# A first projection that reads a feature-major copy of x, in a two-block transformer kernel

## The chip, the cores and the metric

The kernel runs on one core of a Trainium2 chip. Its engines are TensorE (PE; its weight loads stand apart as PEld), VectorE (DVE), ScalarE (ACT), GpSimd (POOL) and SyncE (SP), which here issues the DMAs. The metric is the device time in microseconds (us) of one execution, as the median of several runs; shorter is better.

## The reference, cut to what matters

One sequence of 256 tokens of 1024 features passes two blocks. The part around the change is the first layer of the first block, in which a norm, one wide product and two attentions follow each other:

```python
def rms_norm(x, g):
    xf = x.astype(f32)
    y = xf * lax.rsqrt(jnp.mean(xf * xf, axis=-1, keepdims=True) + EPS)
    return (y * g.astype(f32)).astype(x.dtype)

def even_layer(x, g_norm, w_in, b_f, w_out):
    z = rms_norm(x, g_norm) @ w_in      # q, k, v, gate of 16 "a" heads, 16 forget gates, q, k, v, gate of 16 "b" heads
    ...
def forgetting_attention(q, k, v, log_f):        # the "a" heads
    c = jnp.cumsum(log_f, axis=1).transpose(0, 2, 1)
    ...
        s = s + c[:, :, q0:e, None] - c[:, :, None, :e]
        p = jax.nn.softmax(jnp.where(causal, s, NEG), axis=-1)
```

`log_f` is the log of the sigmoid of the forget product plus a bias. Each head's output is multiplied by its gate (gate times sigmoid of gate) and the result goes through `w_out` and is added to x. After it come a retention layer (block one) and, in block two, a state-space mixer, a sliding-window attention and a gated feed-forward layer.

## The kernel before, in words

A framework schedules the instructions: each engine's list is fixed when the kernel is built, and an engine works through its list in order. The program is one long row of TensorE products on weights that stream in. The class `Weights` loads tiles of 128 x 1024 float32 (512 KB) in the order of use, five raw tiles at a time, and splits each in two: ScalarE casts the raw tile into `wh` (L73), VectorE subtracts it into `wl` (L78). The casts run two tiles ahead of the products, and there are six `wh` and six `wl` tiles. Activations have two parts as well (`xTh`, `xTl`, feature-major: 128 features by 8 feature tiles by 256 tokens), and a product is the sum of three: h by h, h by l, l by h.

The start: `load_x` loads x (four pieces of 256 KB) and the first weight tile; the gain row is spread over 128 partitions by two products (L598) into two PSUM banks. `norm_transposed` forms the squares' sums (ScalarE and VectorE), the factor r with a power on GpSimd, and `xn` = x r g on VectorE (L215). Sixteen TensorE transposes (L235) turn it into PSUM, from where ScalarE casts `xTh` (L242) and VectorE forms `xTl` (L243). `first_xs` is the first projection (v of the first 8 "a" heads, four weight tiles): 48 products of 512 columns, 32 at L289 and 16 with the weights' lower parts at L296. Two of the first four lower weight parts are made by GpSimd. The forget product (24 products of 16 rows, L250 to L252) follows.

Then per half (`hf`) of an attention and per group of four heads (`i`): a q, a k and a gate projection (`proj_ws`: 48 products of 256 columns each), q scaled by ScalarE (L664), k copied by VectorE (L667), the gate through ScalarE's tanh (L670) and VectorE (L671). Each of two pairs of heads then takes: scores (L338) in the two PSUM banks `at`; a masked minimum on VectorE (`masked_min`, L346 and L348); exponentials on ScalarE (`exps`, L355 and L356); a scaling on VectorE (L685, L686); transposes of p (L362) into one of the two PSUM banks `pt`, emptied by ScalarE (`p_transposed`, L364); p by v (L372) in bank `py`.

The mask of the "a" heads comes from the forget gates by a chain: bias and log sigmoid (L630 to L635), a scan over the tokens on VectorE (L637), a reordering copy on GpSimd (L639), a DMA to memory (`c_dram`), a DMA per pair that spreads it over the partitions (`m`), and two additions of the causal mask on GpSimd (L648, L649).

Beside this, VectorE, ScalarE and GpSimd make tables for block two's state space (`trig`, `pw_r`, `m`, L389 to L531), from the parameters `ssm_par`; ScalarE's sines need another function table than its exponentials, and each change is an `ACT_TABLE_LOAD`.

## Time and profile before

| what | value |
|---|---|
| device time, median of 3 runs | 811.92 us |
| lowest and highest run | 810.0 and 812.02 us |
| span of the profiled execution | 810.7 us |
| TensorE products: busy, share of the span | 780.7 us, 96% |
| VectorE | 560.7 us, 69% |
| ScalarE | 408.3 us, 50% |
| GpSimd | 237.2 us, 29% |

The span runs from the first to the last recorded instruction of one profiled execution; the page gives no device time of that execution, so the three runs' times stand beside it. A busy share is an average over the whole program and tells nothing of a single stage.

### The profile page before, as it was taken

The page shows a single profiled execution, that of the slowest core. Times are in us where ns is not written, and L with a number is a line of the kernel's source. Part 1 is how long each engine was busy: PE and PEld are TensorE (multiplying, and loading weights), DVE is VectorE, ACT ScalarE, POOL GpSimd, SP SyncE. Part 2 cuts the span into 40 slices and gives each one's busy share as a digit, 9 for nine tenths or more (in the row PEclk, how much of TensorE's full clock was granted, in tenths as well). Part 3 has the DMA queues.
Part 4 walks back from the last instruction along what each step waited for, and adds up shares of the span by engine and source line. Part 5 has one row for each costly group of instructions (what it writes and reads, how often), then busy time and mean ns, then how long its engine had stood idle before and what let it go on. Part 6 is the DMA issues. An engine that isn't in the chain of part 4 may idle for free.

```text
span 810.7 us, 13533 instructions
## 1 busy us (share of the span) xinstructions
PE 780.7 (96%) x5114; PEld 682.1 (84%) x5114; DVE 560.7 (69%) x1013; ACT 408.3 (50%) x680; POOL 237.2 (29%) x274
## 2 busy tenths in 40 slices
PE   7989999999999999999999999989798999999996
PEld 5978997998997789898989887876577999999886
DVE  6987668678778468585766757698849856565433
ACT  5766565457455355344444355736645544443331
POOL 4662111013604212120202006853653322221110
PEclk9999999999999999999999999999999999999999
DMA  7687544644744757453636494852243765555431
GB/s 284 222 270 234 172 165 131 208 150 154 238 161 133 234 186 254 154 188 124 208 119 194 151 334 152 301 195 85 81 127 110 235 200 177 189 183 181 156 130 53
DMA packets 47427, 146.46 MB, mean 181 GB/s; under 512 B 5361, under 2 KB 11777, under 8 KB 47362
## 3 DMA queue, kind: packets, MB, share of 16 engines
q1 hardware_dynamic: 47362, 145.60, 54.5%
q8 instruction: 40, 0.66, 0.3%
q14 instruction: 25, 0.20, 0.1%
HBM read 137.70 MB, written 7.88 MB: 180 GB/s over the span
## 4 chain that ended last, share of the span: by engine, by line
PE 82%; DVE 5%; POOL 4%; issue 3%; ACT 3%; DMA 3%; SPq 0%; POOLq 0%; DVEq 0%; ACTq 0%
PE bpp L274 12%; PE bpp L275 12%; PE bpp L278 12%; PE bpp L251 9%; PE bpp L250 9%; PE bpp L252 9%; PE bat L252 3%; PE bat L251 3%; PE bat L250 3%; PE bpy L372 2%; PE bat L338 2%; PE bpt L362 1%; PE bpp L289 1%; DVE wl L78 1%; POOL wl L78 1%
## 5 line engine op out<-in xcount | busy, mean ns | idle before, releaser
L78 DVE TENSOR_TENSOR wl<-wraw,wh 128x1024 fp32r<-128x1024 f32 x211 | 276.5, 1321 | 114.9 <-ACT wh L73 114.9
L73 ACT CAST wh<-wraw 128x1024 fp32r<-128x1024 f32 (+1 forms) x233 | 238.6, 1045 | 190.0 <-PE bpp L251 54.1
L251 PE MATMUL bpp<-xTl,wh 128*128 128x256 f32 (+1 forms) x680 | 193.3, 284 | 0.0
L250 PE MATMUL bpp<-xTh,wh 128*128 128x256 f32 (+1 forms) x680 | 193.1, 284 | 0.0
L252 PE MATMUL bpp<-xTh,wl 128*128 128x256 f32 (+1 forms) x680 | 192.9, 284 | 0.0
L251 PEld LDWEIGHTS bpp<-xTl,wh 128*128 128x128 f32 (+1 forms) x680 | 127.3, 187 | 2.6 <-issue 1.9
L250 PEld LDWEIGHTS bpp<-xTh,wh 128*128 128x128 f32 (+1 forms) x680 | 127.3, 187 | 1.8 <-issue 1.3
L252 PEld LDWEIGHTS bpp<-xTh,wl 128*128 128x128 f32 (+1 forms) x680 | 127.3, 187 | 1.0 <-issue 0.8
L274 PE MATMUL bpp<-wh,xTh 128*128 128x512 f32 (+1 forms) x288 | 110.9, 391 | 0.8 <-ACT xTh L242 0.8
L275 PE MATMUL bpp<-wl,xTh 128*128 128x512 f32 (+1 forms) x288 | 109.6, 385 | 0.0
L78 POOL TENSOR_TENSOR wl<-wraw,wh 128x1024 fp32r<-128x1024 f32 x22 | 57.7, 2624 | 62.9 <-ACT wh L73 62.9
L278 PE MATMUL bpp<-wh,xTl 128*128 128x512 f32 (+1 forms) x288 | 74.2, 382 | 0.0
L274 PEld LDWEIGHTS bpp<-wh,xTh 128*128 128x128 f32 x288 | 54.5, 190 | 13.3 <-ACT xTh L242 1.7
L275 PEld LDWEIGHTS bpp<-wl,xTh 128*128 128x128 f32 x288 | 54.5, 189 | 11.1 <-DVE wl L78 0.6
L278 PEld LDWEIGHTS bpp<-wh,xTl 128*128 128x128 f32 x288 | 52.2, 188 | 11.1
L274 PE MATMUL bpp<-wh,yh 128*128 128x512 f32 x128 | 50.5, 400 | 0.0
L275 PE MATMUL bpp<-wl,yh 128*128 128x512 f32 x128 | 50.4, 396 | 0.0
L252 PE MATMUL bat<-xTh,wl 128*128 128x256 f32 x160 | 45.1, 282 | 0.0
L250 PE MATMUL bat<-xTh,wh 128*128 128x256 f32 x160 | 45.1, 282 | 0.0
L251 PE MATMUL bat<-xTl,wh 128*128 128x256 f32 x160 | 45.0, 281 | 0.0
L1119 POOL TENSOR_TENSOR gr<-gr,Rh 128x512 f32<-128x512 f32 x10 | 14.3, 1427 | 75.5 <-ACT th L1118 75.5
L278 PE MATMUL bpp<-wh,yl 128*128 128x512 f32 x128 | 35.6, 395 | 0.0
(380 smaller groups left out, 1312.3 us busy)
## 6 DMA issues: line engine op xcount, KB each, us to landing
wraw<-in_w_o SPq DMA_DIRECT2D x40, 512.0 KB, 4.3
wraw<-in_w_gate SPq DMA_DIRECT2D x22, 512.0 KB, 3.8
wraw<-in_w_up SPq DMA_DIRECT2D x22, 512.0 KB, 4.2
wraw<-in_w_dn SPq DMA_DIRECT2D x22, 512.0 KB, 3.7
wraw<-in_w_v SPq DMA_DIRECT2D x16, 512.0 KB, 4.6
wraw<-in_w_g SPq DMA_DIRECT2D x16, 512.0 KB, 4.4
wraw<-in_w_q SPq DMA_DIRECT2D x12, 512.0 KB, 4.1
wraw<-in_w_va SPq DMA_DIRECT2D x8, 512.0 KB, 6.6
```

Of the source, the lines that this page charges most:

```text
L73: i = nc.scalar.copy(h[:, :n], r[:, :n])
L78: self.lows.append(eng.tensor_tensor(lo[:, :n], r[:, :n], h[:, :n].bitcast(F32), op=ALU.subtract))
L250: T.matmul(ps, lh, rh, start=first, stop=False)
L251: T.matmul(ps, lh, rl, start=False, stop=False)
L252: T.matmul(ps, ll, rh, start=False, stop=last)
L274: T.matmul(ps, lh[:, k0 + k, st], wh, start=first and k == 0, stop=False)
L275: T.matmul(ps, lh[:, k0 + k, st], wl, start=False, stop=False)
L278: T.matmul(ps, ll[:, k0 + k, st], wh, start=False, stop=last and k == n - 1)
L289: m = T.matmul(ps[t], xp[:, k, st], tiles[k // 2][0][:, 512 * (k % 2):512 * (k % 2) + 512], start=xp is xTh and k == 0, stop=False)
L338: i = T.matmul(ps[j][:, o], q[rows, qs], k[rows, ks], start=True, stop=True)
L372: i = T.matmul(o[64 * j:64 * j + 64], v[:, b, vc], src, start=b == 0, stop=b == 1)
L1119: G.tensor_tensor(two(gr), two(gr), rep2(Rh), op=ALU.mult)
```

## The change

The host hands over x a second time, feature-major (`xT`), and the gain as a column per feature tile (`g_col`). ScalarE forms `xTh` = xT g and VectorE `xTl` directly from it, without the norm's factor, and the transposes, the gain's spreading and the row-major norm at the start are gone. The factor of a token, r, is made beside the products: squares of xT on ScalarE behind the fifth cast, sums on VectorE, two products with one column (L693 of the new kernel), the power on GpSimd; a row of factors `R` on every partition comes from two products (L706) behind the first q projection and a ScalarE copy (L708). v takes r in its scaling (L724), the forget product, q, k and the gate are multiplied by R on VectorE (L650, L730, L733, L741), in all passes of both attentions; q's scaling thereby leaves ScalarE.

The first eight weight tiles are loaded into the space of `yh`, `yl`, a ninth into the ordinary raw tiles, the first in two halves between pieces of xT. `first_xs` goes weight tile by weight tile over both token tiles. No lower part of the first projection is made by GpSimd. The forget product uses bank `py`. The row-major x (1 MB) and the masks are loaded behind later weight tiles, and `ssm_par` behind the thirteenth, so the tables begin later. Behind this layer the order of the instructions hardly changes.

```diff
 class Weights:
...
+        self.issued, self.given, self.casts = [], {}, []
...
     def load(self):
         ap = self.jobs[self.loads]
+        n = ap.shape[1]
+        if self.loads in self.given:
+            r = self.given.pop(self.loads)
+        else:
+            r = self.raw.tile([P, 1024], F32, tag="raw", name="wraw")
+        parts = 2 if self.loads == 0 else 1
         self.loads += 1
-        r = self.raw.tile([P, 1024], F32, tag="raw", name="wraw")
-        self.nc.sync.dma_start(r[:, :ap.shape[1]], ap)
+        for i in range(parts):
+            sl = slice(i * n // parts, (i + 1) * n // parts)
+            m = self.nc.sync.dma_start(r[:, sl], ap[:, sl])
+            if i == 0 and parts > 1:
+                self.between()
+        self.issued.append(m)
...
-        i = nc.scalar.copy(h[:, :n], r[:, :n])
+        if not self.done:
+            nc.scalar.copy(h[:, :n // 2], r[:, :n // 2])
+            i = nc.scalar.copy(h[:, n // 2:n], r[:, n // 2:n])
+        else:
+            i = nc.scalar.copy(h[:, :n], r[:, :n])
+        self.casts.append(i)
...
+    def issue_after(self, n, i):
+        self.tc.add_manual_dep(i.ins, self.issued[n].ins.name, NOSYNC, reason="order")
...
-    g_row = nrm.tile([P, D], F32, tag="gain", name="g_row")
-    nc.sync.dma_start(g_row[:1, :], a["even_norm"])
+    warm = const.tile([P, 1], F32, name="warm")
+    A.copy(warm, ones[:, :1])
...
+    g_col = const.tile([P, 8], F32, name="g_col")
+    nc.sync.dma_start(g_col, a["even_norm"])
+    xT = [nrm.tile([P, 4, S], F32, tag="gain", name=f"xT{h}") for h in range(2)]
     def load_x(t):
-        for h in range(XH):
-            sl = slice(h * D // XH, (h + 1) * D // XH)
-            nc.sync.dma_start(x[t][:, sl], a["x"][t * P:(t + 1) * P, sl])
-    load_x(0)
+        w.issue_after(10, nc.sync.dma_start(x[t], a["x"][t * P:(t + 1) * P, :]))
+    def load_xT(k, n=2):
+        nc.sync.dma_start(xT[k // 4][:, k % 4:k % 4 + n, :], a["xT"][:, k:k + n, :])
+    load_xT(0, 1)
...
-            w.plan(xs("w_v" + m, hf), SH[0] if m + str(hf) != "a0" else 2)
+            w.plan(xs("w_v" + m, hf), SH[0])
...
-    w.load()
-    load_x(1)
+    early = [ypool.tile([P, 16, S], F32R, tag=n, name="early")[:].rearrange("p a b -> p (a b)").bitcast(F32)
+             for n in ("yh", "yl")]
+    w.given = {j: early[j // 4][:, 1024 * (j % 4):1024 * (j % 4) + 1024] for j in range(8)}
+    w.between = lambda: load_xT(1, 1)
+    for k in (2, 4, 6):
+        w.load()
+        load_xT(k)
+    for _ in range(5):
+        w.load()
...
-    def first_xs(mid):
-        tiles = [w.next() for _ in range(4)]
+    def first_xs():
         ps = [bank("pp"), bank("pp")]
-        for t in range(2):
-            st = slice(t * P, (t + 1) * P)
-            for g in range(0, 8, 2):
-                for xp in (xTh, xTl):
-                    for k in range(g, g + 2):
-                        m = T.matmul(ps[t], xp[:, k, st], tiles[k // 2][0][:, 512 * (k % 2):512 * (k % 2) + 512],
-                                     start=xp is xTh and k == 0, stop=False)
-                        if t == 0 and xp is xTh and k == 1:
-                            mid(m)
-        for t in range(2):
-            st = slice(t * P, (t + 1) * P)
-            for k in range(8):
-                T.matmul(ps[t], xTh[:, k, st], tiles[k // 2][1][:, 512 * (k % 2):512 * (k % 2) + 512],
-                         start=False, stop=k == 7)
+        tiles = []
+        def part(g, xp, j, first=False, last=False):
+            for k in range(g, g + 2):
+                for t in range(2):
+                    T.matmul(ps[t], xp[:, k, t * P:(t + 1) * P],
+                             tiles[k // 2][j][:, 512 * (k % 2):512 * (k % 2) + 512],
+                             start=first and k == g, stop=last and k == g + 1)
+        for g in range(0, 8, 2):
+            tiles.append(w.next())
+            part(g, xTh, 0, first=g == 0)
+            part(g, xTl, 0)
+            if g:
+                part(g - 2, xTh, 1)
+        part(6, xTh, 1, last=True)
         return ps
...
-        nc.sync.dma_start(sp, a["ssm_par"])
+        w.issue_after(12, nc.sync.dma_start(sp, a["ssm_par"]))
...
-    g_even = [bank("at") for h in range(2)]
-    for h in range(2):
-        T.matmul(g_even[h], ones[:1, :], g_row[:1, h * 512:(h + 1) * 512], start=True, stop=True)
-    norm_transposed(0, g_even, xTh, xTl, "e0", eng=V)
-    def second_tile(after):
-        norm_transposed(1, g_even, xTh, xTl, "e1", KE, None, after)
+    for k in range(8):
+        xk = xT[k // 4][:, k % 4, :]
+        A.activation(xTh[:, k, :], xk, AF.Copy, scale=g_col[:, k:k + 1])
+        V.scalar_tensor_tensor(xTl[:, k, :], xk, g_col[:, k:k + 1], xTh[:, k, :].bitcast(F32),
+                               op0=ALU.mult, op1=ALU.subtract)
...
-            ps = bank("pp")
+        def forget_product():
+            ps = bank("py")
             wf = [y.rearrange("p (k c) -> p k c", c=16) for y in w.next()]
...
+            V.tensor_tensor(az, ps[:16, :S], R[:16, :], op=ALU.mult)
...
+        rh = []
+        R = evc.tile([P, S], F32, name="Re")
+        def square_sums():
+            sq = [ev.tile([P, 512], F32, tag=n, name="sq_e") for n in ("q", "k", "q", "k")]
+            for j in range(4):
+                i = A.activation(sq[j], xT[j // 2][:, 2 * (j % 2):2 * (j % 2) + 2, :].rearrange("p a b -> p (a b)"),
+                                 AF.Square, scale=1.0 / math.sqrt(D))
+                tc.add_manual_dep(i.ins, w.casts[4].ins.name, NOSYNC, reason="order")
+            V.tensor_tensor(sq[0], sq[0], sq[1], op=ALU.add)
+            V.tensor_tensor(sq[2], sq[2], sq[3], op=ALU.add)
+            V.tensor_tensor(sq[0], sq[0], sq[2], op=ALU.add)
+            V.tensor_tensor(sq[1][:, :S], sq[0][:, :S], sq[0][:, S:], op=ALU.add)
+            return sq[1][:, :S]
+        def norm_factors(sm):
+            pr = bank("pt")
+            rs = []
+            for t in range(2):
+                T.matmul(pr[:, t:t + 1], sm[:, t * P:(t + 1) * P], ones[:, :1], start=True, stop=True)
+            for t in range(2):
+                rs.append(rstd_from([pr[:, t:t + 1]], EPS, "e"))
+                rh.append(evc.tile([P, 1], F32, name=f"rh{t}"))
+                V.tensor_scalar(rh[t], rs[t], 0.5, None, op0=ALU.mult)
+            return rs
+        def factor_row(rs, after):
+            pr = bank("pt")
+            for t in range(2):
+                rb = ev3.tile([P, P], F32, tag="s", bufs=5, name="rb_e")
+                V.tensor_copy(rb, rs[t].to_broadcast([P, P]))
+                i = T.matmul(pr[:, t * P:(t + 1) * P], rb, ident, start=True, stop=True)
+                tc.add_manual_dep(i.ins, after.ins.name, NOSYNC, reason="order")
+            A.copy(R, pr[:, :S])
...
-                ps = proj_xs(xTh, xTl, 8) if mi or hf else first_xs(second_tile)
+                if mi or hf:
+                    ps = proj_xs(xTh, xTl, 8)
+                else:
+                    ps = first_xs()
+                    pf = forget_product()
+                    rs = norm_factors(square_sums())
+                    p0 = proj_ws()
+                    factor_row(rs, last_mm[-1])
...
-                    A.mul(v[:, t, :], ps[t], 0.5)
+                    A.mul(v[:, t, :], ps[t], rh[t])
...
-                    A.mul(q.rearrange("p a b -> p (a b)"), ps, -0.125)
+                    V.scalar_tensor_tensor(q, rows(ps), -0.125, rep2(R), op0=ALU.mult, op1=ALU.mult)
...
-                    V.tensor_copy(k.rearrange("p a b -> p (a b)"), ps)
+                    V.tensor_tensor(k, rows(ps), rep2(R), op=ALU.mult)
+                    if not (mi or hf or i):
+                        w.issue_after(6, nc.sync.dma_start(masks, a["c_masks"]))
+                        for t in range(2):
+                            load_x(t)
...
-                    A.activation(gs, ps, AF.Tanh, scale=0.5)
-                    V.scalar_tensor_tensor(gs, gs, 1.0, ps, op0=ALU.add, op1=ALU.mult)
+                    gr = ev.tile([P, 2 * S], F32, tag="gr", bufs=1, name="gr_e")
+                    V.tensor_tensor(rows(gr), rows(ps), rep2(R), op=ALU.mult)
+                    A.activation(gs, gr, AF.Tanh, scale=0.5)
+                    V.scalar_tensor_tensor(gs, gs, 1.0, gr, op0=ALU.add, op1=ALU.mult)
...
     a["x"] = c(i["x"][0][ORDER])
-    a["even_norm"] = c(i["even_norm"][0])
+    a["xT"] = c(a["x"].T.reshape(8, P, S).transpose(1, 0, 2))
+    a["even_norm"] = c(i["even_norm"][0].reshape(8, P).T)
```

**TensorE at the start.** These are TensorE's first rows before; `bpp` is the projection's PSUM bank, and a count is of like instructions in a row.

```order
L598 MATMUL bat<-g_row,ones 128x512 x2
L235 MATMUL bpt<-ident,xn 128x128 x8
L289 MATMUL bpp<-wh,xTh 128x512 x2
L289 MATMUL bpp<-wh,xTl 128x512 x2
L235 MATMUL bpp<-ident,xn 128x128 x4
L289 MATMUL bpp<-wh,xTh 128x512 x2
L289 MATMUL bpp<-wh,xTl 128x512 x2
L235 MATMUL bpy<-ident,xn 128x128 x4
```

The same place of the changed kernel:

```order
L308 MATMUL bpp<-wh,xTh 128x512 x4
L308 MATMUL bpp<-wh,xTl 128x512 x4
L308 MATMUL bpp<-wh,xTh 128x512 x4
L308 MATMUL bpp<-wh,xTl 128x512 x4
L308 MATMUL bpp<-wl,xTh 128x512 x4
L308 MATMUL bpp<-wh,xTh 128x512 x4
L308 MATMUL bpp<-wh,xTl 128x512 x4
L308 MATMUL bpp<-wl,xTh 128x512 x4
```

Transposes and the gain's products are gone, each weight tile is used for both token tiles (four products per part), and a tile's lower part comes in one tile later.

**ScalarE at the pairs of the first half.** Before, ScalarE's rows from the first tanh to the copies of the second pair's transposed p; `trig` are the sines of the tables, `s,dn<-s,nm` the exponentials.

```order
L461 ACT_TABLE_LOAD
L461 ACTIVATE trig<-trig 128x1024 x2
L73 CAST wh<-wraw 128x1024
L355 ACT_TABLE_LOAD
L355 ACTIVATE s,dn<-s,nm 128x128 x2
L73 CAST wh<-wraw 128x1024
L356 ACTIVATE s,dn<-s,nm 128x256
L664 ACTIVATE q<-bpp 128x512
L356 ACTIVATE s,dn<-s,nm 128x256
L355 ACTIVATE s,dn<-s,nm 128x128
L356 ACTIVATE s,dn<-s,nm 128x256
```

In the changed kernel, these are the rows of the third pair of heads up to the copy (L385) that empties the bank of the second pair's first transposed p:

```order
L376 ACTIVATE s,dn<-s,nm 128x128
L377 ACTIVATE s,dn<-s,nm 128x256
L482 ACT_TABLE_LOAD
L482 ACTIVATE trig<-trig 128x1024
L376 ACT_TABLE_LOAD
L376 ACTIVATE s,dn<-s,nm 128x128
L377 ACTIVATE s,dn<-s,nm 128x256
L86 CAST wh<-wraw 128x1024 x2
L482 ACT_TABLE_LOAD
L482 ACTIVATE trig<-trig 128x1024
L347 CAST yh<-o 128x256
L385 COPY pT<-bpt 128x384
```

The two sines have moved from ahead of the first pair's exponentials to between and behind those of the third pair, with three table loads, and the copy of p stands behind them.

**VectorE between the first and the third pair.** In the changed kernel, a piece of VectorE's list behind the second pair's masked minimum (`ISA s,nm`), up to the third pair's; of before, nothing of the tables' `trig` stands between these pairs, since it lies ahead of the first.

```order
L410 SCALAR_TENSOR_TENSOR trig<-trig 128x512 x2
L92 TENSOR_TENSOR wl<-wraw,wh 128x1024
L741 TENSOR_TENSOR gr_e<-bpp,Re 128x512
L506 TENSOR_TENSOR sm_t_1690<-pw_r,pw_i 128x16
L507 TENSOR_TENSOR sm_t_1691<-pw_i,pw_r 128x16
L525 TENSOR_TENSOR sm_fr<-sm_u_1717,sm_u_1718 128x16
L92 TENSOR_TENSOR wl<-wraw,wh 128x1024
L756 RECIPROCAL rd<-dn 128x2
L414 SCALAR_TENSOR_TENSOR trig<-trig 128x512 x2
```

The tables' work now lies on VectorE among the pairs' own instructions.

## Rows read from the trace of the kernel before

A row of a timeline gives: start in us, duration, engine, line, operation, out<-in, shapes, count, and in brackets the idle time before it and what ended it.

**Rows 1.** The profile's page: its first line, the products' row under heading 1 (busy time, share of the span, instructions), and under heading 4 the shares by engine of the chain of work that ended last.

```profile
span 810.7 us, 13533 instructions
...
PE 780.7 (96%) x5114; PEld 682.1 (84%) x5114; DVE 560.7 (69%) x1013; ACT 408.3 (50%) x680; POOL 237.2 (29%) x274
...
PE 82%; DVE 5%; POOL 4%; issue 3%; ACT 3%; DMA 3%; SPq 0%; POOLq 0%; DVEq 0%; ACTq 0%
```

**Rows 2.** Who TensorE waited for between 11 and 110 us: total us, times, longest.

```profile
PE bat L338 <- DVE nm L348: 1.8, 1, 1.8
PE bpt L362 <- DVE s L685: 1.6, 1, 1.6
```

**Rows 3.** Busy time by stretch of the start; a row is start:end in us, its length, then busy time and instructions of PE, PEld, DVE, ACT and POOL, the granted TensorE clock, the DMA share and GB/s.

```profile
0.00:11.07 11.07, 5.71 (x13) 2.73 (x13) 4.63 (x15) 4.81 (x10) 3.18 (x14) 1.00 0.73 265
...
25.33:45.38 20.05, 20.05 (x171) 19.50 (x169) 20.05 (x40) 12.85 (x15) 15.68 (x11) 1.00 0.63 193
```

**Rows 4.** The timeline of the first 26 us, from ScalarE's, TensorE's, GpSimd's and VectorE's lists.

```profile
4.18 0.63 ACT L202 ACTIVATE junk<-x 128x512 bf16<-128x512 f32 x1 [2.18 <-DMA x<-in_x]
8.27 1.05 ACT L73 CAST wh<-wraw 128x1024 fp32r<-128x1024 f32 x1 [3.37 <-DMA wraw<-in_w_va]
...
11.07 1.22 PE L289 MATMUL bpp<-wh,xTh 128*128 128x512 f32 x2 [1.74 <-ACT xTh L242]
12.09 1.05 PE L289 MATMUL bpp<-wh,xTl 128*128 128x512 f32 x2
12.94 1.05 PE L235 MATMUL bpp<-ident,xn 128*128 128x128 f32 x4
...
14.65 0.76 PE L289 MATMUL bpp<-wh,xTl 128*128 128x512 f32 x2
...
16.15 0.63 PE L289 MATMUL bpp<-wh,xTl 128*128 128x512 f32 x2
16.61 1.10 PE L289 MATMUL bpp<-wh,xTh 128*128 128x512 f32 x4
...
25.33 0.28 PE L250 MATMUL bpp<-xTh,wh 128*16 128x256 f32 x1
...
12.52 2.38 POOL L78 TENSOR_TENSOR wl<-wraw,wh 128x1024 fp32r<-128x1024 f32 x1 [1.15 <-ACT wh L73]
13.57 2.41 DVE L78 TENSOR_TENSOR wl<-wraw,wh 128x1024 fp32r<-128x1024 f32 x1
```

**Rows 5.** The timeline of the DMA queue (SPq): three of its issues.

```profile
8.26 0.34 SPq L623 DMA_DIRECT2D masks<-in_c_masks  x1
...
10.85 0.33 SPq L407 DMA_DIRECT2D pos_i<-in_positions  x1
...
13.53 2.81 SPq L63 DMA_DIRECT2D wraw<-in_w_qa  x2
```

**Rows 6.** The mask chain: lists of GpSimd, VectorE and the DMA queue, 34 to 55 us.

```profile
34.85 5.57 POOL L530 COPY m<-sm_mag 128x256 f32<-128x256 f32 x1 [0.43 <-DMA w_dram<-m]
...
42.87 0.67 DVE L637 TENSOR_TENSOR_SCAN c_f<-ones,z_f 16x256 f32<-16x256 f32 x1
43.60 2.27 POOL L639 COPY c_f<-c_f 16x256 f32<-16x256 f32 x1 [1.20 <-DVE c_f L637]
...
54.64 0.29 DVE L346 CUSTOM_DVE_ANT_0 s<-bat,m 128x128 f32<-128x128 f32 x1 [3.73 <-POOL m L648]
```

**Rows 7.** ScalarE's list: a table load and the instruction behind it, a sine pair, a log-gate chain, an exponential.

```profile
26.67 1.28 ACT L461 ACT_TABLE_LOAD   x1
27.96 0.26 ACT L461 ACTIVATE sm_trig<-sm_trig 128x64 f32<-128x64 f32 x1
...
36.84 1.28 ACT L634 ACT_TABLE_LOAD   x1
38.13 0.51 ACT L634 ACTIVATE az_f<-az_f,ones 16x256 f32<-16x256 f32 x1
...
49.70 2.01 ACT L461 ACTIVATE trig<-trig 128x1024 f32<-128x1024 f32 x2
...
72.09 0.40 ACT L355 ACTIVATE s<-s,nm 128x128 f32<-128x128 f32 x1 [0.29 <-DVE nm L346]
```

**Rows 8.** Groups of VectorE's instructions between 25 and 105 us by line and shape: busy us, mean ns of one (ends of neighbours overlap a little), idle before.

```profile
L78 DVE TENSOR_TENSOR wl<-wraw,wh 128x1024 fp32r<-128x1024 f32 x26 | 33.0, 1275 | 9.3 <-ACT wh L73 9.3
L389 DVE SCALAR_TENSOR_TENSOR trig<-trig 128x512 f32<-128x512 f32 x6 | 4.0, 672 | 0.0
...
L671 DVE SCALAR_TENSOR_TENSOR gs<-gs,bpp 128x512 f32<-128x512 f32 x2 | 1.3, 672 | 0.0
```

**Rows 9.** TensorE's list at the end of the first half's pairs: transposes, p by v, and the scores that open the second half's pairs.

```profile
84.54 0.49 PE L362 MATMUL bpt<-ident,s 128*128 128x128 f32 x3
84.96 0.87 PE L372 MATMUL bpy<-pT,v 128*64 128x256 f32 x8
85.76 0.55 PE L362 MATMUL bpt<-ident,s 128*128 128x128 f32 x3
...
104.55 0.93 PE L338 MATMUL bat<-k,q 64*128 64x128 f32 x8
```

**Rows 10.** Busy time by stretch around 580 us, columns as in rows 3.

```profile
578.00:581.50 3.50, 1.31 (x10) 1.07 (x10) 3.47 (x4) 1.40 (x4) 1.54 (x2) 1.00 0.00 0
581.50:584.90 3.40, 3.19 (x12) 2.13 (x13) 3.40 (x6) 3.40 (x8) 3.14 (x3) 0.51 0.74 272
```

More of the change, by code (lines that the diff above doesn't have):

```diff
@@ L36 @@
 SH = (0, 0, 2, 8)
-KE = ("pp", "py")
-XH = 2
 KO = (("pt", "pt"), ("at", "at"))
@@ L203, in mean_square @@
         return s
-    def norm_transposed(t, g, th, tl, name, kinds=("pt", "pt"), eng=None, after=None):
-        with tc.high_priority():
-            xt = x[t]
-            parts = [mean_square(xt[:, h * 512:(h + 1) * 512], D, name, eng if h else None) for h in range(2)]
-            r = rstd_from(parts, EPS, name)
-            xn = []
-            for h in range(2):
-                sl = slice(h * 512, (h + 1) * 512)
-                xn.append(nrm.tile([P, 512], F32, tag="xn", bufs=3, name="xn"))
-                V.scalar_tensor_tensor(xn[h], xt[:, sl], r, g[h], op0=ALU.mult, op1=ALU.mult)
-            return transposed(xn, 8, th, tl, 0, t, kinds, after)
     def gained_transposed(t, g, kinds):
@@ L227, in gained_transposed, with transposed @@
         return transposed(xn, 8, xTh, xTl, 0, t, kinds)
-    def transposed(src, n, th, tl, k0, t, kinds=("pt", "pt"), after=None):
+    def transposed(src, n, th, tl, k0, t, kinds=("pt", "pt")):
         m = min(4, n)
@@ L234, in transposed @@
             for j in range(m):
-                i = T.transpose(pt[:, j * P:(j + 1) * P], sb[:, j * P:(j + 1) * P], ident)
-                if after is not None:
-                    tc.add_manual_dep(i.ins, after.ins.name, NOSYNC, reason="order")
-                    after = None
+                T.transpose(pt[:, j * P:(j + 1) * P], sb[:, j * P:(j + 1) * P], ident)
             pv = pt[:, :m * P].rearrange("p (j t) -> p j t", j=m)
@@ L251, in mm3 @@
         T.matmul(ps, lh, rl, start=False, stop=False)
-        T.matmul(ps, ll, rh, start=False, stop=last)
+        last_mm[:] = [T.matmul(ps, ll, rh, start=False, stop=last)]
     def proj_ws(kind="pp"):
@@ L618, in model_kernel @@
         c_dram = dram.tile([16, S], F32, name="c_dram")
-        def forget_gates():
-            nc.sync.dma_start(bf, a["even_b_f"])
-            nc.sync.dma_start(masks, a["c_masks"])
-            ps = bank("pp")
+        def forget_product():
+            ps = bank("py")
             wf = [y.rearrange("p (k c) -> p k c", c=16) for y in w.next()]
@@ L652, in model_kernel @@
+        rows = lambda y: y.rearrange("p (a b) -> p a b", a=2)
+        rep2 = lambda y: y[:, None, :].to_broadcast([P, 2, S])
         for mi, m in enumerate(("a", "b")):
             for hf in range(2):
-                ps = proj_xs(xTh, xTl, 8) if mi or hf else first_xs(second_tile)
+                if mi or hf:
[6 more added lines that the diff above has]
+                    factor_row(rs, last_mm[-1])
```

16 lines of the change are left out of this document (9 added, 7 removed).

## The prediction

> **What bounds the kernel now.** I read the page first. TensorE is busy for 780.7 of 810.7 us, and the chain that ended last lies on it for 82% [rows 1]: a change can only win by removing time in which TensorE does nothing needed, or does it slowly. So I went to the list of TensorE's waits next, from the first projection to 110 us, and it holds two of any size apart from the start: 1.8 us at the second pair's scores, which need a PSUM bank that VectorE's masked minimum gives back, and 1.6 us at the first pair's transposes, which need VectorE's scaled p [rows 2]. Both hang on the first mask: the first masked minimum begins at 54.64, after 3.73 us in which VectorE had nothing else to do [rows 6]. Last I read the stretch ahead of it. TensorE's first useful product starts at 11.07 and the first projection ends at 25.33 [rows 4], and there the speed matters. Between 12.09 and 12.94 two products of 512 columns take 0.85 us, 0.43 each; from 16.15 to 16.61 two take 0.46, 0.23 each [rows 4]. That is TensorE's lower level, 1.2 GHz, until about 14.65, some 3.6 us after steady work began, and then the higher. (The granted-clock column prints 1.00 for the first stretch [rows 3]; I go by the steps.) Later a product of 256 columns takes 20.05 / 171 = 0.117 us [rows 3].
>
> **The change, step by step: the first projection.** The same bytes have to come, 1.05 MB of x and 2.1 MB in four weight tiles. In the DMA queue an issue follows the landing of the eighth issue before it, which gives arrival times: the issue at 8.26 follows the first weight tile (1.05 MB in), that at 10.85 the second (2.1 MB), that at 13.53 the fourth (3.1 MB) [rows 5]; the first quarter MB of x was there at 4.18 [rows 4]. Now the first half tile has only 0.13 MB of x ahead of it: on the line through these points it is there at 4.9, bounds 4.5 and 6.6, and the first product follows its cast at 5.2 to 7.2. The second tile is complete with 1.57 MB, so at 9.6, and cast at 10.6 (1.05 us a cast [rows 4]). Until then TensorE has eight products, 3.4 us at the low level, which ends by then; 40 products at 0.234 follow, with the third and fourth tile (12.2, 13.53) in time. That ends at 10.6 + 9.4 = 20.0; with 0.4 for pauses I take 20.4. Bounds: 18.3 if only the fourth tile waits (13.53 + 1.05 + 16 x 0.234), and 22.0 if the 3.6 us at the low level start only at 10.6 (8.4 products lose 0.196 each). Lead: 25.33 - 20.4 = 4.9.
>
> **What is added on TensorE.** Two products for the factor row, 128 columns each, bounded by the transposes of like shape, 0.42 / 3 = 0.14 [rows 9]: 0.3. Two products with one column: between nothing and 0.1; I take 0.1. Lead 4.5. TensorE's list is otherwise the old one up to the scores at 104.55 [rows 9]; it has fewer transposes.
>
> **What is added elsewhere and hidden.** Two lower weight parts leave GpSimd, where one took 2.38 beside a VectorE part of 2.41 [rows 4], for VectorE at 1.28 [rows 8]: four parts and the four pairs of xTl fit beside 13 us of products. Squares (4 x 0.6), sums and the power lie beside the forget product and the first q projection, 72 x 0.117 = 8.4 us; the factor is needed when v frees the banks, at 28.9, and I have it ready at 26 (squares by 19, four sums of up to 0.67 between weight parts, a power). The later loads of x and masks are needed after 45 us; 1.3 MB at 265 GB/s [rows 3] are 5 us. Per pass, q and the gate's extra multiplication put 1.3 us on VectorE (0.67 each [rows 8]), which has idle time in a pass (69% busy [rows 1]). In the passes behind the first half I cost this at nothing: TensorE waited for nothing there [rows 2]. Without that cover it would be 8 x 1.3 = 10 us, the worst end of this item; I see no row for it.
>
> **The two waits go.** The pairs' work stands later in TensorE's list: the second pair's scores by about 25 products, the first transposes by about 50. So the first mask may come some 3 us later relative to TensorE before the 1.8 and 1.6 return. That adds 3.4: a gain of 7.9 if no new wait appears, and the scores at 104.55 then stand at 96.6.
>
> **A new wait.** Now the mask. The forget product needs R: 20.4 + 72 x 0.117 + 0.3 + 0.35 for its copy = 29.4. ScalarE's exponential of the gates stands behind a cast that gets its tile when three quarters of the k projection are done, at 33.1; cast, exponential, table load (1.28) and logarithm (0.51) [rows 7] end at 36.4; VectorE's list then has two weight parts and small table work ahead of the scan: it ends at 39.8. From the scan's end to the first masked minimum, before: 54.64 - 43.54 = 11.1 (GpSimd's copy 2.27, two DMAs, an addition [rows 6]). So the first masked minimum starts at 50.9, with one weight part (1.2) either way, and moving with the end of the first projection. That is early enough for the two waits above. But behind it VectorE's list has five weight parts (1.13 from start to start), eight `trig` instructions (0.60), q, k, the gate's two, and the pairs' own: 19.7 us up to the third pair's masked minimum. Then ScalarE's list: the third pair's exponentials (1.9), three table loads (3.9), two sines (2.0), two casts (2.0), a cast of y, and only then the copy that empties the second pair's PSUM bank: 10.4 us [rows 7, 8]. It ends at 50.9 + 30.1 = 81.0. TensorE comes to the transposes that need this bank 18.3 us before the scores at 96.6 (124 products of 0.117, three p by v of 0.80, four triples of transposes at 0.30 to 0.42 [rows 9]): at 78.3. It waits for 2.7.
>
> A rule speaks for a longer wait. The load row ends at 26.67 + 1.28 = 27.95 and the sine behind it starts at 27.96 [rows 7], so I count 1.28 a load. By the Trainium skill, "ScalarE: Activation LUTs", section "What ACT_TABLE_LOAD costs", a switch costs 2.66 us, since a drain of 1.38 belongs to it; the trace disagrees, and by the page the wait would be 2.7 + 3 x 1.38 = 6.8.
>
> **Sum.** 4.5 + 3.4 - 2.7 = 5.2 us. On the profiled span 810.7 - 5.2 = 805.5; the median of the runs lies 1.2 above that span, so **806.7**. Own range 804 to 809.5: the first projection's end (-2.1, +1.6) and a weight part (1.2) in the mask chain.
>
> **Rivals.** (a) No new wait: if the mask comes 2.7 us earlier relative to TensorE than I have it, which is two weight parts less between R and the third pair, or if ScalarE's copy does not stand on the path as I read it, the wait is gone. Gain 7.9, **804.0**. For it: GpSimd and VectorE have no tables to make ahead of the scan, and 11.1 us from the scan to the masked minimum may be long. (b) On the other side: GpSimd's copies stretch beside VectorE. A copy `m` took 5.57 at 34.85, and the gates' copy 2.27 for an eighth of its partitions [rows 6]. The changed list has a copy `m` right ahead of the gates' copy; at 5.57 it is over 3.8 us after the scan's end, and the gates' own copy at 5.57 adds 3.3. The first masked minimum comes at 58.0, each us of it is a us of TensorE, **813.8**. It decides from 56.1 (no gain left), and against it stands that in the trace of before the gates' own copy, with VectorE just as busy, took 2.27. (c) The clock: at 578 TensorE was busy for 1.31 of 3.5 us, and the next 3.40 us were granted 0.51, the lower level [rows 10]. If TensorE's pauses between arriving weight tiles do the same here, all 48 products take 0.43: 7.2 + 20.6 = 27.8 in place of 20.4, and **814.1**. Against it: from 10.6 no pause is left in my sum. The Trainium skill, "TensorE: Matmul & The Clock Gate", section "HAM oscillation — how this bites in real kernels", describes this, waits for DMA between groups of products that drop the clock each time. (d) By the drain of table loads the wait is 4.1 longer: **810.8**; no row here bears it out.
>
> **How the numbers follow.** Forecast 0.50, (a) 0.25, (b) 0.17, (c) 0.05, (d) 0.03. About 0.3%, 2.4 us, is what a measurement can tell from no change: faster means under 809.5, slower over 814.3. Nearly all of the forecast and (a) are faster: 0.70. (b) spreads over 809 to 816 as its copies stretch little or much; with it, (c), (d) and the forecast's upper end, 0.18 are within, and 0.12 slower. The range from 803 to 812 leaves out half of (b), (c) and a tail of (a).
>
> **What would show it.** The first projection's end at 20.4, with steps of 0.43 for its first eight products and 0.23 after; no wait of TensorE at the first two pairs; the first masked minimum near 50.9; ScalarE's copy of the second pair at about 81, with two sines just ahead, and TensorE's one wait of some 3 us there; nothing new behind 105 us. Wrong would make it: VectorE's extra 1.3 us a pass showing as waits in later passes; R late, so that v holds the PSUM banks; `ssm_par` landing after 34 and holding ScalarE's list ahead of the gates' exponential.

## The result, and the profile after

The changed kernel is slower: 817.88 us as the median of 4 runs (816.51 to 819.6) against 811.19 for the kernel before on the same chip, a ratio of 1.0082 (95% interval 1.0061 to 1.0102). On another chip, beside part of the experiments, it took 815.59 against 812.92: 1.0043 (1.0025 to 1.0062). The forecast was 806.7, faster, in a range of 803 to 812. The profiled execution took 816.51 with a span of 814.7. One execution of all, the first profiled one of the kernel with late sines, took 1532 us, with 0.45 to 0.47 us for a product of 512 columns throughout; it is in none of the comparisons.

The page of the changed kernel, its first line and the products' row, as [rows 1] before:

```profile
span 814.7 us, 13536 instructions
...
PE 782.8 (96%) x5102; PEld 684.5 (84%) x5102; DVE 570.4 (70%) x1038; ACT 411.2 (50%) x679; POOL 212.9 (26%) x272
```

Busy time says little: 2 us more for TensorE though it has 12 recorded products fewer. The list of TensorE's waits from the start to 130 us (total us, times, longest) answers to [rows 2]:

```profile
PE bpp L308 <- ACT wh L83: 5.2, 1, 5.2
PE bpt L383 <- ACT pT L385: 4.3, 1, 4.3
PE bpp L308 <- ACT wh L84: 1.5, 1, 1.5
PE bpp L308 <- ACT wh L86: 1.1, 1, 1.1
```

Both waits of [rows 2] are gone. Three waits for a cast weight tile stand at the start, and there is one new wait of 4.3 us, at the transposes (L383), for ScalarE's copy out of their bank (L385).

The start on TensorE, as [rows 4] (start, duration, count; 512 columns each):

```profile
5.23 1.22 PE L308 MATMUL bpp<-wh,xTh 128*128 128x512 f32 x2 [5.23 <-ACT wh L83]
7.96 1.22 PE L308 MATMUL bpp<-wh,xTh 128*128 128x512 f32 x2 [1.51 <-ACT wh L84]
8.97 1.91 PE L308 MATMUL bpp<-wh,xTl 128*128 128x512 f32 x4
11.96 2.08 PE L308 MATMUL bpp<-wh,xTh 128*128 128x512 f32 x4 [1.08 <-ACT wh L86]
...
15.55 1.87 PE L308 MATMUL bpp<-wl,xTh 128*128 128x512 f32 x4
17.25 1.10 PE L308 MATMUL bpp<-wh,xTh 128*128 128x512 f32 x4
...
23.06 1.09 PE L308 MATMUL bpp<-wl,xTh 128*128 128x512 f32 x4
```

The first product starts at 5.23, but four products still take 1.7 us from 15.55 to 17.25: TensorE is at its lower level, 1.2 GHz, until 17.25, where that ended at 14.65 before. Only then do four take 0.94. The projection ends at 24.0 (25.33 before). ScalarE's list around the new wait:

```profile
76.08 0.40 ACT L376 ACTIVATE s<-s,nm 128x128 f32<-128x128 f32 x1 [3.94 <-DVE nm L367]
...
77.08 1.28 ACT L482 ACT_TABLE_LOAD   x1
78.38 1.06 ACT L482 ACTIVATE trig<-trig 128x1024 f32<-128x1024 f32 x1
79.45 1.28 ACT L376 ACT_TABLE_LOAD   x1
...
81.64 1.98 ACT L86 CAST wh<-wraw 128x1024 fp32r<-128x1024 f32 x2
83.64 1.28 ACT L482 ACT_TABLE_LOAD   x1
84.93 1.06 ACT L482 ACTIVATE trig<-trig 128x1024 f32<-128x1024 f32 x1
85.89 0.39 ACT L347 CAST yh<-o 128x256 fp32r<-128x256 f32 x1
86.19 0.47 ACT L385 COPY pT<-bpt 128x384 f32<-128x384 f32 x1
```

And TensorE there, with the stretch's busy times and granted clock under it (columns as [rows 3]):

```profile
82.14 0.28 PE L270 MATMUL bpp<-xTl,wh 128*128 128x256 f32 x1
86.71 0.90 PE L383 MATMUL bpt<-ident,s 128*128 128x128 f32 x3 [4.29 <-ACT pT L385]
...
87.63 0.41 PE L269 MATMUL bpp<-xTh,wh 128*128 128x256 f32 x1
87.84 0.41 PE L270 MATMUL bpp<-xTl,wh 128*128 128x256 f32 x1
```

```profile
78.00:86.00 8.00, 4.42 (x33) 3.41 (x31) 5.95 (x21) 7.93 (x12) 1.70 (x3) 0.97 0.52 163
86.00:90.00 4.00, 3.29 (x16) 3.29 (x17) 3.90 (x13) 3.98 (x7) 0.20 (x1) 0.50 0.69 204
90.00:95.00 5.00, 5.00 (x35) 4.49 (x35) 2.83 (x8) 4.99 (x13) 1.48 (x2) 0.77 0.95 290
```

ScalarE works without a pause from 77 to 86 (7.93 of 8.00 us busy), on three table loads and two sines among other things, and the copy is the last of it. Behind the wait the granted clock is 0.50, and a product of 256 columns takes 0.21 us in place of 0.12 until about 92. The wait is paid one and a half times.

The balance, on the spans. At 35 us the changed kernel is 0.2 ahead (1.3 from the first projection's end; less 0.7 for the factor's products and some tenths around). The two old waits give 3.4. The new wait takes 4.3, and some 24 products and three transposes at the low clock take 2.6 more than they would. That makes 3.3 behind; the scores that stood at 104.55 [rows 9] start 3.8 later. From there to the end the distance stays between 3.7 and 4.1. This balance explains the 4.0 us between the two profiled executions; the medians are 6.7 apart, the profiled execution of after was the fastest of its four, that of before slower than any of its listed runs, and no trace shows the other 2.7.

### The profile page after: what moved, and what is told of

It reads as the page before. It is cut to its first block, busy times and chain, and to the rows that moved or that the text cites. A ratio compares the mean times of both kernels' runs of the same rounds, so it can differ in the third digit from the quotient of the medians.

```text
span 814.7 us, 13536 instructions
## 1 busy us (share of the span) xinstructions
PE 782.8 (96%) x5102; PEld 684.5 (84%) x5102; DVE 570.4 (70%) x1038; ACT 411.2 (50%) x679; POOL 212.9 (26%) x272
## 5 line engine op out<-in xcount | busy, mean ns | idle before, releaser
L92 DVE TENSOR_TENSOR wl<-wraw,wh 128x1024 fp32r<-128x1024 f32 x205 | 268.5, 1320 | 103.8 <-ACT wh L86 103.4
L86 ACT CAST wh<-wraw 128x1024 fp32r<-128x1024 f32 x225 | 231.4, 1047 | 190.3 <-PE bpp L270 57.4
L271 PE MATMUL bpp<-xTh,wl 128*128 128x256 f32 x672 | 192.6, 287 | 0.0
L269 PE MATMUL bpp<-xTh,wh 128*128 128x256 f32 x672 | 192.2, 286 | 0.0
L270 PE MATMUL bpp<-xTl,wh 128*128 128x256 f32 x672 | 191.7, 285 | 0.0
L269 PEld LDWEIGHTS bpp<-xTh,wh 128*128 128x128 f32 x672 | 127.8, 190 | 2.2 <-issue 1.8
L271 PEld LDWEIGHTS bpp<-xTh,wl 128*128 128x128 f32 x672 | 127.7, 190 | 1.5 <-issue 1.5
L270 PEld LDWEIGHTS bpp<-xTl,wh 128*128 128x128 f32 x672 | 127.8, 190 | 1.0 <-issue 0.7
L92 POOL TENSOR_TENSOR wl<-wraw,wh 128x1024 fp32r<-128x1024 f32 x20 | 51.3, 2564 | 60.8 <-ACT wh L86 60.7
L294 PEld LDWEIGHTS bpp<-wl,xTh 128*128 128x128 f32 x288 | 54.9, 191 | 11.1 <-DVE wl L92 0.6
```

Source lines behind the costliest of these rows:

```text
L86: i = nc.scalar.copy(h[:, :n], r[:, :n])
L92: self.lows.append(eng.tensor_tensor(lo[:, :n], r[:, :n], h[:, :n].bitcast(F32), op=ALU.subtract))
L269: T.matmul(ps, lh, rh, start=first, stop=False)
L270: T.matmul(ps, lh, rl, start=False, stop=False)
L271: last_mm[:] = [T.matmul(ps, ll, rh, start=False, stop=last)]
L294: T.matmul(ps, lh[:, k0 + k, st], wl, start=False, stop=False)
```

## The experiments

The theories: **T**, the late tables put sines and table loads ahead of the copy that TensorE waits for, and the wait brings the clock down; **S**, at the start TensorE's pauses between arriving tiles keep it at the lower level; **V**, the rival, VectorE's added products by R are what makes the pairs late.

The first run with late sines, the products of ones, the two together and the late tables in the kernel before were measured on one chip, the others on a second, each beside runs of the kernel before. Across the two chips the ratios to before are what can be compared. Inside the traces one landmark serves: the scores that before start at 104.55 [rows 9].

**Late sines.** One edit: the two sines are ordered behind the last copy of the first half.

```diff
+    copies = []
...
-        return o, A.copy(o, pt[:, :3 * P])
+        copies.append(A.copy(o, pt[:, :3 * P]))
+        return o, copies[-1]
...
         for t in trig + [sm]:
-            A.activation(t, t, AF.Sin)
+            i = A.activation(t, t, AF.Sin)
+            if t is not sm:
+                tc.add_manual_dep(i.ins, copies[7].ins.name, NOSYNC, reason="order")
```

> Only ScalarE's two sines of the tables are moved behind the last copy of p of the first half (behind about 90 us); VectorE's list and the start stay as in the changed kernel. Theory T (the two sines and their three table loads ahead of the copy that empties the bank are what TensorE waits 4.3 us for, and the lower clock behind the wait costs 2.5 more): the copy ends by 81, no wait, granted clock 1.00 from 80 to 95, about 811 us (817.9 less 7). Rival V (VectorE's products by R make the third pair late): VectorE's list is unchanged, the wait stays, 817 to 818 us.

> The run with late sines once more, since its profiled execution ran at the low clock from end to end. Theory T: no wait of TensorE between 60 and 100 us and granted clock 1.00 there, 810 to 811 us; first projection's end near 24 as in the changed kernel, since its start is the same.

Measured: 810.53 (0.9964 of before, 0.9945 to 0.9983) and, once more, 809.10 (0.9953, 0.9937 to 0.9969), that is 6.5 us less than the changed kernel on the same chip (815.59, below). TensorE's waits from 11 to 110 us in the second, and two stretches:

```profile
PE bpt L385 <- DVE s L762: 1.0, 1, 1.0
PE bpp L308 <- ACT wh L86: 0.8, 1, 0.8
```

```profile
80.00:85.00 5.00, 4.04 (x35) 3.42 (x34) 5.00 (x12) 2.77 (x4) 1.88 (x3) 1.00 0.43 137
85.00:90.00 5.00, 5.00 (x45) 4.54 (x44) 4.89 (x19) 4.39 (x13) 0.20 (x1) 1.00 0.86 238
```

The wait for the copy is gone and the clock stays at 1.00; what is left is 1.0 us for VectorE. The two profiles on that chip have the same start (the first projection ends at 23.0 in both, against the expected 24), and at the landmark, the changed kernel's row first, the late sines are 5.4 ahead:

```profile
106.92 0.93 PE L359 MATMUL bat<-k,q 64*128 64x128 f32 x8
```

```profile
101.54 0.93 PE L359 MATMUL bat<-k,q 64*128 64x128 f32 x8
```

VectorE's own work was not reduced. T holds, and V alone is not the cause of this wait. V's share in its length is not shown: the stretch of ScalarE's list that ends in the copy starts from VectorE's masked minimum of the third pair, and no run leaves out R with the sines in the changed kernel's place.

**Products of ones at the start.** Products of a matrix of ones into a bank that nobody reads, 14 ahead of the first product, 6 and 4 in the pauses: 24 in all, not the 26 of the expectation. The trace has two records of each, and the framework put 16, 4 and 4 at these places.

```diff
+        def idle(n):
+            for _ in range(n):
+                T.matmul(pw[:, :P], ones, ones, start=True, stop=True)
+        pw = bank("at")
+        idle(14)
         for g in range(0, 8, 2):
             tiles.append(w.next())
+            if g == 2:
+                idle(4)
...
             for k in range(g, g + 2):
+                if k == 1 and xp is xTh and j == 0:
+                    idle(6)
```

> 26 products of a matrix of ones that nobody reads are put on TensorE ahead of the first product and into the pauses between the first weight tiles. Theory S (TensorE stays at 1.2 GHz up to 17.25 because it pauses between arriving tiles): the steps of 512 columns are 0.23 from the second weight tile on (about 12 us), the first projection ends at 21.3 in place of 24.0. Rival (the low level lasts until about 17 whatever TensorE does): it ends at 24 or later. The framework puts the sines of the tables elsewhere in this build, ahead of the third pair's exponentials, with two table loads fewer between, so its total, 811 to 816 us, does not speak for the start alone.

Measured: 808.42 (0.9938, 0.9917 to 0.9959), the first projection's end at 21.3. The total is below the 811 to 816 that was expected, but the sines moved as well in this build: no wait for a copy is longer than 0.6. The next run has these products and the late sines, the edits of both.

> The products of ones and the sines behind the first half's pairs together. To be held against the run with late sines alone, which has nearly the same ScalarE list. Theories S and T together: first projection ends at 21.3, no wait and no lower clock at 80 to 95, about 808 us. If S falls: 811 us as with late sines alone. If T falls: 815 us or more.

Measured: 809.17 (0.9951, 0.9932 to 0.9970). Both runs have the steps that were expected; the rows of the second:

```profile
8.52 1.09 PE L310 MATMUL bpp<-wh,xTl 128*128 128x512 f32 x4
9.44 1.06 PE L316 MATMUL bat<-ones 128*128 128x128 f32 x8
11.02 1.20 PE L310 MATMUL bpp<-wh,xTh 128*128 128x512 f32 x4 [0.53 <-ACT wh L86]
...
19.61 1.10 PE L310 MATMUL bpp<-wl,xTh 128*128 128x512 f32 x4
```

Four products take 0.92 from 8.52 on, and the projection ends at 20.6. What fills the pauses is useless work, and it is worth 1.7 to 3.4 us there (21.3 and 20.6 against 23.0 and 24.0). At the landmark the run with both, at 98.19, is 3.4 ahead of late sines alone; the framework arranged its lists anew too, so not all of this is the start's. But the total is not 3.4 below that of late sines alone (809.10, 810.53): 0 to 1.4. The run with both lost 2.7 us of its lead at 555 to 620 us, a stretch that the edits don't touch (last section).

**Ones at the head alone.** As the run with both, without the ones in the pauses.

```diff
-            if g == 2:
-                idle(4)
...
-                if k == 1 and xp is xTh and j == 0:
-                    idle(6)
```

> Late sines, and the products of ones only ahead of the first product (14), none in the pauses between weight tiles. It asks whether the pauses themselves (1.5 and 1.1 us) bring the clock down or keep it down. If steady work at the head is enough: steps of 0.23 from about 6 to 8 us on and an end of the first projection near 21, 809 us. If the pauses hold the clock low: steps of 0.43 until about 17 and an end near 24, 811 us.

Measured: 809.34 (0.9958, 0.9943 to 0.9974), end of the first projection at 23.0.

```profile
8.62 1.10 PE L308 MATMUL bpp<-wh,xTl 128*128 128x512 f32 x4
11.82 1.19 PE L308 MATMUL bpp<-wh,xTh 128*128 128x512 f32 x4 [2.10 <-ACT wh L86]
12.85 1.73 PE L308 MATMUL bpp<-wh,xTl 128*128 128x512 f32 x4
14.38 1.91 PE L308 MATMUL bpp<-wl,xTh 128*128 128x512 f32 x4
```

```profile
12.00:17.00 5.00, 5.00 (x16) 3.92 (x17) 5.00 (x8) 4.75 (x10) 0.00 (x0) 0.66 1.04 415
```

Neither expectation fits alone. The clock is up at 8.62 (0.23 a product), holds over the first product group behind a pause of 2.1, and falls then: 0.66 granted, 0.43 a product until about 16. So steady work at the head raises the clock, and behind the pauses, of 0.7 and 2.1, it falls again, as it does not in the run with both, where they are filled: S, in both directions. Up to the landmark (101.57) the lists are otherwise those of late sines alone, and so is the first projection's end: the ones at the head alone gained nothing.

**Late tables in the kernel before.** One part of the change done alone, with the load behind the eleventh weight tile (the thirteenth in the change).

```diff
+        self.issued = []
...
-        self.nc.sync.dma_start(r[:, :ap.shape[1]], ap)
+        self.issued.append(self.nc.sync.dma_start(r[:, :ap.shape[1]], ap))
...
-        nc.sync.dma_start(sp, a["ssm_par"])
+        i = nc.sync.dma_start(sp, a["ssm_par"])
+        tc.add_manual_dep(i.ins, w.issued[10].ins.name, NOSYNC, reason="order")
```

> The kernel before, with nothing changed but that the parameters of the tables are loaded behind the eleventh weight tile, so that the sines come among the first half's pairs. Theory T: late tables alone cost time, by a wait of TensorE of 2 to 5 us for a copy of p or for VectorE between 60 and 90 us and a lower clock behind it: 814 to 819 us. If the changed kernel's loss comes from its start and VectorE's additions: 811 to 812 us, no change.

Measured: 816.62 (1.0046, 1.0031 to 1.0062), 4.2 more than before. In the even layer the trace loses 1.8 of it: a wait of 1.4 for a copy of p behind a sine, and a lower clock behind that.

```profile
69.21 0.87 PE L373 MATMUL bpy<-pT,v 128*64 128x256 f32 x8 [1.35 <-ACT pT L365]
```

```profile
70.00:75.00 5.00, 5.00 (x19) 3.73 (x18) 4.58 (x14) 4.66 (x11) 1.13 (x1) 0.66 0.98 332
```

The other 2.9 of that profiled execution fall in the stretch at 555 to 620 us again. So late tables alone do harm by the same mechanism, but this run shows only 1.8 us of it for certain.

**The yardstick, and the factor's products.** The changed kernel once more beside these runs, and the run with both without the multiplications of q, k and the gate by R.

```diff
-                    V.scalar_tensor_tensor(q, rows(ps), -0.125, rep2(R), op0=ALU.mult, op1=ALU.mult)
+                    A.mul(q.rearrange("p a b -> p (a b)"), ps, -0.125)
...
-                    V.tensor_tensor(k, rows(ps), rep2(R), op=ALU.mult)
+                    V.tensor_copy(k.rearrange("p a b -> p (a b)"), ps)
...
-                    V.tensor_tensor(rows(gr), rows(ps), rep2(R), op=ALU.mult)
-                    A.activation(gs, gr, AF.Tanh, scale=0.5)
-                    V.scalar_tensor_tensor(gs, gs, 1.0, gr, op0=ALU.add, op1=ALU.mult)
+                    A.activation(gs, ps, AF.Tanh, scale=0.5)
+                    V.scalar_tensor_tensor(gs, gs, 1.0, ps, op0=ALU.add, op1=ALU.mult)
```

> The changed kernel unchanged, on the chip of the runs beside it, as their yardstick: about 818 us, a wait of 4 us for ScalarE's copy of p near 82 and a granted clock of about 0.5 behind it, first projection's end near 24.

Measured: 815.59; the same wait of 4.3, granted clock 0.69 from 85 to 90, and an end of the first projection at 23.0, since the clock rose at 15.3 and not at 17.25. The scores at the landmark are 2.4 behind the kernel before, where they were 3.8 behind in the first profile. The start differs by 1 us between these two executions of one kernel.

> Products of ones and late sines, and q, k and the gate are not multiplied by the norm's factor (that factor is left out there): q is scaled by ScalarE, k copied, the gate read from the bank, as in the kernel before. It measures what VectorE's added products cost by themselves. My theory (VectorE has the time in its passes): as with both, 809 us, within 1 us. Rival V (VectorE is late and TensorE waits for it in the passes): 3 to 10 us less.

Measured: 809.78 (0.9969, 0.9954 to 0.9984) against 809.17 (0.9951) with them on the other chip. At the landmark the run without them is at 100.07, behind the 98.19 with them. VectorE's 1.3 us a pass cost nothing that can be seen here, with the sines moved away: V finds no support.

**Early tables.** The parameters' load is written ahead of the layer's loop, and stands behind the eighth weight tile in the queue.

```diff
-        sp = pool.tile([P, 1140], F32, name="ssm_par")
-        w.issue_after(12, nc.sync.dma_start(sp, a["ssm_par"]))
+        sp = par_early[0]
...
         c_dram = dram.tile([16, S], F32, name="c_dram")
+        par_early.append(tab.tile([P, 1140], F32, name="ssm_par"))
+        w.issue_after(4, nc.sync.dma_start(par_early[0], a["ssm_par"]))
```

> The changed kernel with one thing undone: the tables' parameters are loaded behind the eighth weight tile, not the thirteenth (ScalarE's list then has the sines between the second and the third pair, and one table load fewer around them). Theory T: the wait of 4.3 us for the copy of p behind the sines is gone or under 1.5, no lower clock behind it, 809 to 812 us. Rival (the place of the sines does not matter, any order waits as long): 815 us or more.

Measured: 811.63 (1.0001, 0.9982 to 1.0021), 4.0 less than the changed kernel's 815.59 on the same chip, by the ratios 0.42%. The two sines stand together at 67.9, one copy of p behind them; TensorE's waits to 110 us:

```profile
PE bat L360 <- DVE nm L370: 1.9, 1, 1.9
PE bpp L308 <- ACT wh L86: 1.6, 1, 1.6
```

The wait for the copy is gone, and the old one for the second pair's minimum is back, with a lower clock behind it:

```profile
57.00:60.50 3.50, 3.50 (x18) 3.37 (x17) 3.50 (x8) 1.89 (x3) 1.02 (x1) 0.52 0.66 210
```

Not all of the 4.0 is T's. In this execution the first tile's second half came earlier (its cast starts at 6.02, not 7.3), so that eight products ran without a pause, and from 11.18 on four take 1.03 and then 0.93, with no ones in the list:

```profile
5.45 2.46 PE L308 MATMUL bpp<-wh,xTh 128*128 128x512 f32 x4 [5.45 <-ACT wh L83]
...
11.18 1.19 PE L308 MATMUL bpp<-wh,xTh 128*128 128x512 f32 x4 [1.64 <-ACT wh L86]
```

The first projection ends at 20.8, 2.1 to 3.2 before the changed kernel's; at the landmark the run is at 101.0, 5.9 ahead of the changed kernel's 106.92. The edit leaves the queue up to there as it was, so this is the execution's luck, and it speaks for S: without the pause inside the first tile the higher level is there in time, and the pause of 1.64 does not end it. With the products of ones added:

> Early parameters and the products of ones together, the sines again ahead of the first pair as in the kernel before. Theories S and T: first projection's end near 20.6, 807 to 809 us, the best of the builds.

Measured: 809.29 (0.9953, 0.9936 to 0.9969). Expected as the best, it is not: within 1 us of the others that have neither the wait nor the low start.

**Ones in the kernel before: a miss.**

```diff
+    pw = bank("py")
+    for _ in range(16):
+        T.matmul(pw[:, :P], ones, ones, start=True, stop=True)
     norm_transposed(0, g_even, xTh, xTl, "e0", eng=V)
...
         ps = [bank("pp"), bank("pp")]
+        for _ in range(10):
+            T.matmul(ps[0][:, :P], ones, ones, start=True, stop=True)
```

> The kernel before with 26 products of ones ahead of the transposes and the first product. It asks how much of the gain of the other runs comes from the clock alone. Theory S: its first eight products take 0.23 in place of 0.43, 1 to 2 us less than before (811 on a chip where before takes 812.9), so that most of the changed kernel's possible gain is its own. Rival (all of the gain is the clock's): 808 to 809.

Measured: 821.35 (1.0118, 1.0069 to 1.0167). The framework arranged the list anew and put scores earlier:

```profile
PE bat L340 <- DVE nm L350: 7.0, 1, 7.0
PE bat L340 <- DVE k L672: 2.8, 1, 2.8
```

TensorE stood 9.8 us before the masks were there. How much of the gain the clock alone would give the kernel before stays open.

**GpSimd's share back.** To the run with both:

```diff
-            w.plan(xs("w_v" + m, hf), SH[0])
+            w.plan(xs("w_v" + m, hf), SH[0] if m + str(hf) != "a0" else 2)
```

> Products of ones and late sines, and two of the first projection's four lower weight parts are made by GpSimd again. My sum held the move of these parts to VectorE for free either way: within 1 us of the run with both, 809 us. Rival (GpSimd beside VectorE slows both, as the 2.4 us parts of before suggest, and the projection waits for a lower part): 1 to 3 us more, a wait at a product with a lower part.

Measured: 809.75 (0.9963, 0.9945 to 0.9981) against 809.17: no difference in the total that can be told. The two runs are from different chips; by the ratios, 0.9963 and 0.9951, it is the same. GpSimd's two parts take 2.42 each, and the first projection ends at 21.2 in place of 20.6.

## Why the prediction was wrong

- **What bounds the kernel**: right. TensorE's waits, its clock and 0.7 us of added products make up the balance on the spans, to some 0.5 us.
- **The first projection ends at 20.4**: wrong, 24.0 (23.0 in the second profile). This is the first step that failed. My line through arrival times had the second tile at 9.6; its cast started on landing at 10.87, and the products at 11.96 instead of 10.6. And I let the low level end ahead of the second tile ("which ends by then"), as if the two pauses ahead of that tile did not count. They did: it lasted to 17.25, so that twelve products which I priced at 0.234 took 0.44, 2.5 us. With the pauses filled the end was 20.6 and 21.3 (the second tile's cast started at 9.93 and 10.66 there), and 20.8 in the run with early parameters, so the rest of the term was sound. My rival (c) named this mechanism with a chance of 0.05, though it took all 48 products for slow where 20 were; and my argument against it, that no pause is left from 10.6 on, looked behind the pauses and not at them.
- **The two waits go**: right, no wait at the first two pairs.
- **The new wait**: its place, its bank and its cause were right, its size was not: 4.3 for 2.7. The first masked minimum came at 53.7 for 50.9, 2.8 late with a first projection that was 3.6 late. That it was no later is luck: the scan ended at 44.2 for 39.8, and the way from there to the minimum took 9.5 for 11.1. VectorE's list from the first to the third pair's minimum took 22.0 for 19.7; ScalarE's took 10.6 for 10.4. TensorE came there at 82.4 for 78.3.
- **What the wait costs behind it**: missing from the sum, and the step that turns the sign together with the first projection. The products behind the wait ran at 0.50 of the clock for some 5 us: 2.6 us. I had the row for it, [rows 10], and used it for the start alone. The Trainium skill, "TensorE: Matmul & The Clock Gate", section "HAM oscillation — how this bites in real kernels", says of a loop whose groups of products wait for DMA that each next group starts cold. The trace agrees for this wait, which was for ScalarE and not for DMA: 4.3 us of waiting were followed by 0.50, and the run with late sines, without the wait, has 1.00 there.
- **Hidden additions**: right as far as it was tested. VectorE's products by R, with the sines moved away, and the lower parts taken from GpSimd cost nothing that a run could tell, and TensorE has no wait for the late loads of x and the masks. The late load of `ssm_par` is another matter: it is what put the sines where they cost.
- **Rival (a)**, no new wait: fell. The wait came, and longer.
- **Rival (b)**, GpSimd's copies stretching: fell. The copy of the gates took 0.65 and the one ahead of it 0.40:

```profile
43.25 0.40 POOL L551 COPY m<-sm_mag 128x256 f32<-128x256 f32 x1 [13.37 <-DVE sm_mag L547]
44.32 0.65 POOL L659 COPY c_f<-c_f 16x256 f32<-16x256 f32 x1 [0.67 <-DVE sm_trig L410]
```

- **Rival (d)**, a drain behind each table load: fell. The load at 77.08 takes 1.28 and the sine starts at 78.38.
- **The total**: on the spans 805.5 was forecast and 814.7 came: 3.6 from the first projection, 1.6 from the wait, 2.6 from the clock behind it, 0.3 from the factor's products, about 1 unplaced. Also, a device time is 1.8 above its span in this kernel's runs (816.51 and 814.7), so the profile of before stands for 812.5, above its highest listed run and not at the median: 0.6 of the forecast.

A version beats both kernels: the changed one with products of ones in the pauses (and the sines where the framework then put them) takes 808.42, 0.9938 of before; with late sines alone it takes 809 to 811.

## What to carry to other kernels

Price a wait of TensorE twice: the time of the wait, and the products behind it at half the clock, if the profile has one place where a pause was followed by a lower granted clock. Not every wait is followed by one. In the kernel before, the waits of 1.8 and 1.6 at 56.16 and 61.14 left the clock at 1.00, where the wait of 1.9 in the run with early parameters was followed by 0.52. The row of before:

```profile
55.00:62.00 7.00, 4.23 (x34) 3.68 (x35) 6.83 (x21) 3.27 (x10) 4.51 (x7) 1.00 1.04 350
```

So the second price is a risk to put into the range. When work starts earlier but in pieces that wait for data, do not let the low clock end among the pieces: in the two profiles of the changed kernel it lasted past the last pause, to 17.25 and 15.3, and only a row of a start with such pauses could have told. And when an edit delays side work (tables here), look at which in-order list it lands in and whose bank copy stands behind it; moving that side work behind the pairs gave back the loss.

## What the runs showed of the hardware that was not expected

The granted-clock column prints 1.00 in the first microseconds whatever the steps say: in the changed kernel twelve products of 512 columns fill the 5.25 us below, 0.44 each, under a printed 1.00, where the run with ones at the head has 0.66 for steps of 0.43. The steps are to be trusted there.

```profile
12.00:17.25 5.25, 5.25 (x12) 4.09 (x13) 5.00 (x7) 4.76 (x9) 0.00 (x0) 1.00 1.04 415
```

The stretch from 555 to 620 us, which no edit touches, differs by up to 3.6 us between builds (without the factor's products, against before). The kernel before and the run with both, at the same place:

```profile
610.00:615.00 5.00, 2.20 (x15) 1.73 (x15) 5.00 (x9) 3.46 (x9) 3.27 (x2) 1.00 0.00 2
```

```profile
605.00:610.00 5.00, 2.60 (x15) 1.76 (x13) 5.00 (x8) 2.75 (x8) 3.29 (x2) 0.86 0.03 13
610.00:615.00 5.00, 4.58 (x21) 4.58 (x22) 5.00 (x8) 2.88 (x5) 2.18 (x2) 0.50 0.01 3
```

TensorE stands idle for half of 5 us beside a busy VectorE in both (the run with both is some 5 us earlier there), but the granted clock falls behind it in one of them alone. That bounds what these totals can tell: differences under 3 us between the better builds are not explained here.
